# A two-layer hybrid decoder trunk: 272 projection columns moved from fifth to second place, ones multiplied ahead of the first slab, and float32r rows of 1/rms

## The chip, the cores and the metric

The kernel runs on one core of one Trainium2 chip (trn2). The metric is device time of one launch in microseconds (us), and the runs of the kernel before have a median of 1244.14 us (three runs, 1243.88 to 1245.17).

## The reference

The input is one sequence of 512 tokens with 1024 features, in float32, and it goes through two layers. Layer 0 mixes tokens by gated linear attention (GLA) and by differential attention side by side, layer 1 by dilated window attention; each is followed by a gated MLP. Only layer 0's mixer and the norms matter here:

```python
h = rmsnorm(x, norm_mix[0])
z = h @ w_in                                  # 1024 x 3088 columns
aq, ak, av, ag, ar, bq, bk, bv = split(z)     # 256,256,512,512,16,512,512,512
log_a = log_sigmoid(ar @ w_a2 + b_a) / 16     # decay of the GLA
oa = rmsnorm(gla(aq, ak, av, log_a)) * silu(ag)
ob = rmsnorm(diff_attention(norm(bq), norm(bk), bv, lam))
x = x + concat(oa, ob) @ w_out
x = x + mlp(rmsnorm(x, norm_ffn[0]))          # up to 2*2816, conv of 3, silu gate, down
```

## The kernel before, in words

**Products.** Every weight is split on the chip into a high and a low float32r half (hi by ScalarE, line 177; lo by VectorE, line 180), and so is every activation (hhi by line 204, hlo by line 205). A product is three passes: high times high, low times high, high times low. Weights come in slabs of at most 1088 columns per partition, three buffers each of raw, hi and lo. `slab()` hands out the next one and issues the load of the one two places further, so the order of `weight_slabs()` (line 94) is also the order of the weight transfers on SyncE's queue.

**Layer 0's projection.** `tok_gemm` (lines 303 to 320) makes 512, 272 or 256 columns for all 512 tokens, in four groups of 128 tokens with a PSUM bank each. It goes slab by slab, in each slab token group by token group. A 512-column product has four slabs of 24 matmuls, a 272- or 256-column one has two slabs of 48. The order before (lines 694 to 701) is: bv, bq, bk, aq with ak, half of ag with ar (the 272 columns), av, the other half of ag (256 columns). The last one's final eviction is followed by a Silu of the whole gate on ScalarE (line 686) and by the reload of the table for Ln and Exp (line 687).

**The order of TensorE's work** is written out by hand with a planner. `now` is a planned time; each step of a projection adds its planned cost (`PASS` is 0.216 us for 512 columns), and after each step all small pieces of attention that have come due are issued (`fire`). A piece is put on the list by the piece before it, with a delay in planned time:

```python
FILL, SLOPE, DTR, DPV = 1.2, 0.55, 5.5, 2.5
at(DTR, lambda: diff_tr(n, h, pr[0]), "diff")
at(FILL + SLOPE * (n + 1), lambda: diff_scores(i + 1), "diff")
```

The differential attention is one chain of 16 steps (four token blocks n of four heads), which starts after the transposes of bk. A step has scores (line 493), the transposes of its weights 5.5 later (line 515; ScalarE copies them out, line 518) and the product with bv 2.5 after that (line 527). After a block's fourth head its output is copied out (line 532), normed (lines 348 to 356 and 473) and 7.5 later transposed (line 362) and split. The block n = 3 also starts the GLA chain: `gla_sums` (line 595; ScalarE's exponentials in lines 600 and 601, VectorE's products in lines 606 to 616), `gla_tr` 5.0 later (transposes), `gla_att` (line 631), `gla_out` (lines 659 to 670). The decay needs three small pieces for each token group, `decay1` to `decay3` (lines 557, 565 and 584), started by the eviction of the 272 columns (line 551). Before the first half of the output projection (line 332) stands `drain("diff")`, before its second half `drain("gla")`:

```python
def drain(tag):
    while any(e[2] == tag for e in events):
        e = heapq.heappop(events)
        now[0] = max(now[0], e[0])
        e[3]()
```

It issues every listed piece in order of its due time until none of the tag is left, with no projection step between them. The order on ScalarE and VectorE is not written by hand: a scheduler at build time sets it.

**The start.** x is loaded in eight chunks of 128 features (256 KB each), and the first two are split at once; the first weight slab is loaded and split in two halves, of one chunk each.

**The rows of 1/rms.** Before each MLP the summed squares (128 partitions x 512 tokens, `sqacc`) are added over partitions by one float32 matmul with ones (line 251), whose result goes through a reciprocal root to all rows. It is issued after the first two up-projections (line 720, 48 matmuls).

Of the kernel before, what the change touches and what calls it, by code (L numbers as in the profile page):

```python
# [16 lines left out]
F32 = mybir.dt.float32  # L17
F32R = mybir.dt.float32r
# [6 lines left out]
P = 128  # L25
S = 512
D = 1024
DC = D // P
NT = S // P
# [48 lines left out]
def weight_slabs():  # L78


    slabs = []

    def tok(w, c0, n):
        nk = 2 if n == 512 else 4
        slabs.extend((w, 0, k * P, nk, c0, n) for k in range(0, DC, nk))

    def ffn(i):
        for gi, (f0, n) in enumerate(GROUPS):

            for j in range(f0 + (gi > 0), f0 + n + (gi < 2)):  # L90
                slabs.extend(("ffn_w_up", i, 0, DC, half + j * P, P) for half in (0, DFF))
            slabs.extend(("ffn_w_down", i, f0 * P, n, c * P, P) for c in range(DC))

    for c0, n in ((2576, 512), (1552, 512), (2064, 512), (0, 512), (1280, 272), (512, 512), (1024, 256)):
        tok("ev_w_in", c0, n)
    for r0 in (512, 0):
        slabs.extend(("ev_w_out", 0, r0, 4, c0, 256) for c0 in range(0, D, 256))
    ffn(0)
    for g, kind in ((0, 0), (0, 1), (1, 0), (1, 1), (2, 0), (2, 1), (0, 2), (1, 2), (2, 2)):
        tok("od_w_in", g * 1536 + kind * 512, 512)  # L100
    slabs.extend(("od_w_out", 0, 0, 4, c0, 256) for c0 in range(0, D, 256))
    ffn(1)
    return slabs
# [24 lines left out]
def trunk_kernel(ctx: ExitStack, tc: tile.TileContext, x, weights, params, lqks, w_a2, consts, out):  # L128
    nc = tc.nc
    V, A, G, T = nc.vector, nc.scalar, nc.gpsimd, nc.tensor  # L130

    per = ctx.enter_context(tc.tile_pool(name="per", bufs=1))
# [3 lines left out]
    ps = ctx.enter_context(tc.tile_pool(name="ps", bufs=8, space=PSUM))  # L136
# [4 lines left out]
    def bank():  # L141
        return ps.tile([P, 512], F32, name="bank")
# [64 lines left out]
    def rsqrt(dst, ss, scale, work=None):  # L207
# [7 lines left out]
        V.scalar_tensor_tensor(out=u, in0=u, scalar=-0.5, in1=a, op0=ALU.mult, op1=ALU.mult)  # L215
        V.scalar_tensor_tensor(out=dst, in0=u, scalar=1.5, in1=y, op0=ALU.add, op1=ALU.mult)

    def to_h(c, gain):
        split(hhi[:, c], hlo[:, c], xT[:, c], gain[:, c:c + 1])

    sqacc = [None]
# [23 lines left out]
                self.r = per.tile([P, NT], F32, name="rstd4", bufs=2)  # L245
                rsqrt(self.r, self.pb[:, :NT], 1.0 / D)

    def rstd_rows():

        pb = bank()  # L250
        T.matmul(pb, ones.to_broadcast([P, P]), sqacc[0], start=True, stop=True)
        bc = per.tile([P, S], F32, name="rstd_bc", tag="row", bufs=1)
        a, y, u = (tmp.tile([P, S], F32, name="qn", bufs=3) for _ in range(3))
        rsqrt(bc, pb, 1.0 / D, (a, y, u))
        return bc
# [34 lines left out]
    def run(steps):  # L290
        for us in steps:
            pe(us)
            fire()
# [6 lines left out]

    PASS = 0.216 / 512

    def tok_gemm(n, lhs, evict, before=None):

        ps = [bank() for _ in range(NT)]
        nsl = 4 if n == 512 else 2
        kper = DC // nsl
        for s in range(nsl):
            whi, wlo = slab()
            if before is not None:  # L310
                before(s)
            for t in range(NT):
                for k in range(kper):
                    kc = s * kper + k
                    for j, (a, b) in enumerate(((hhi, whi), (hlo, whi), (hhi, wlo))):
                        T.matmul(ps[t][:, :n], lhs(a[:, kc], t), b[:, k, :n],  # L316
                                 start=(kc == 0 and j == 0), stop=(kc == DC - 1 and j == 2))
                if s == nsl - 1:
                    evict(t, ps[t])
                yield 3 * kper * n * PASS  # L320

    def nat(v, t):
        return v[:, t * P:(t + 1) * P]
# [76 lines left out]
    with tc.tile_pool(name="m0", bufs=1) as m0, tc.tile_pool(name="t0", bufs=2) as t0:  # L400
# [34 lines left out]
        nc.sync.dma_start(prm, params[:, :38])  # L435
        for i in range(4):
            for c in (2 * i, 2 * i + 1):
                nc.sync.dma_start(xT[:, c], x[c])
                if i == 0:
                    to_h(c, gmix[0])  # L440
                    if c == 0:
                        load_next()
            if i in (1, 2):
                load_next()
# [246 lines left out]

            at(8.0, lambda: scaled(bv, r0)(t, ps), "params")

        run(tok_gemm(512, nat, late, before))
        run(tok_gemm(512, nat, qk_evict(qT, g_dqk, 8, r0, "diff")))
        run(tok_gemm(512, nat, qk_evict(kT, None, 8, r0, "diff", after_k)))
        run(tok_gemm(512, nat, scaled(aqk, r0)))
        run(tok_gemm(272, nat, agr_evict))
        oahi, oalo = t8("oahi", F32R), t8("oalo", F32R)
        run(tok_gemm(512, nat, scaled(av, r0, then=landing)))  # L700
        run(tok_gemm(256, nat, agr1_evict))
# [11 lines left out]
    def ffn(i, done):  # L713
        with tc.tile_pool(name=f"f{i}", bufs=2) as fp:
            def up(j):
                whi, wlo = slab()
                ps = bank()
                for kc in range(DC):
                    for m, (w, r) in enumerate(((whi, hhi), (wlo, hhi), (whi, hlo))):
                        T.matmul(ps, w[:, kc], r[:, kc], start=(kc == 0 and m == 0),  # L720
                                 stop=(kc == DC - 1 and m == 2))
                pe(3 * DC * 512 * PASS)
                return ps

            def conv3(ps, j, name):
                u = fp.tile([P, S], F32, name="u" + name)
                c = fp.tile([P, S], F32, name="c" + name)
                V.tensor_tensor(out=u, in0=ps, in1=bc, op=ALU.mult)
                cw = [conv[:, i, q, j:j + 1] for q in range(4)]
                A.activation(c, u, AF.Identity, bias=cw[3], scale=cw[2])  # L730
                V.scalar_tensor_tensor(out=c[:, 1:], in0=u[:, :S - 1], scalar=cw[1], in1=c[:, 1:], op0=ALU.mult,
                                       op1=ALU.add)
                V.scalar_tensor_tensor(out=c[:, 2:], in0=u[:, :S - 2], scalar=cw[0], in1=c[:, 2:], op0=ALU.mult,
                                       op1=ALU.add)
                return c

            ghi, glo = {}, {}

            def gate(j, pg, pv):
                cg = conv3(pg, j, "g")  # L740
                cv = conv3(pv, NF + j, "v")
                silu = A.activation(cg, cg, AF.Silu)
                if j == NF - 1:
                    tc.keep_in_program_order(A.preload_act_table_set(LN_EXP))
                V.tensor_tensor(out=cv, in0=cg, in1=cv, op=ALU.mult)  # L745
                ghi[j] = fp.tile([P, S], F32R, name="ghi", bufs=10)
                glo[j] = fp.tile([P, S], F32R, name="glo", bufs=10)
                split(ghi[j], glo[j], cv, None)

            def chunk(j):  # L750
                pg = up(j)
                gate(j, pg, up(NF + j))
                fire()

            def down(gi):
                f0, n = GROUPS[gi]
                last = gi == len(GROUPS) - 1

                def part(c, w, ps, ks, ts=slice(0, S)):
                    for k in ks:  # L760
                        for m, (a, b) in enumerate(((w[0], ghi), (w[1], ghi), (w[0], glo))):
                            T.matmul(ps[:, ts], a[:, k], b[f0 + k][:, ts], start=(k == 0 and m == 0),  # L762
                                     stop=(k == n - 1 and m == 2))
                    pe(3 * len(ks) * (ts.stop - ts.start) * PASS)

                def end(c, ps, ts=slice(0, S)):
                    V.tensor_tensor(out=xT[:, c, ts], in0=xT[:, c, ts], in1=ps[:, ts], op=ALU.add)  # L767
                    if last:
                        done(c, ts)


                first = min(LEAD, DC) if last else 0
                pend = []
                for c in range(first):
                    w, ps = slab(), bank()
                    part(c, w, ps, range(n - 1))
                    pend.append((c, w, ps))
                for c, w, ps in pend:
                    part(c, w, ps, (n - 1,))
                    end(c, ps)  # L780
                for c in range(first, DC):
                    w = slab()

                    parts = 2 if last and i == 1 and c == DC - 1 else 1
                    for q in range(parts):
                        ps, ts = bank(), slice(q * S // parts, (q + 1) * S // parts)
                        part(c, w, ps, range(n), ts)
                        fire()
                        end(c, ps, ts)

            p0 = up(0), up(NF)
            bc = rstd_rows()
            p1 = up(1), up(NF + 1)
            gate(0, *p0)
            gate(1, *p1)
            for gi, (f0, n) in enumerate(GROUPS):
                for j in range(f0 + (1 if gi else 2), f0 + n + (gi < 2)):
                    chunk(j)
                down(gi)
# [206 lines left out]
```

## Time and profile before

| | |
|---|---|
| median of three runs | 1244.14 us |
| time of the profiled execution | 1244.83 us |
| its span, first to last instruction | 1242.7 us |
| TensorE busy (matmuls) | 1230.5 us, 99% |
| VectorE busy | 765.5 us, 62% |
| ScalarE busy | 542.7 us, 44% |
| DMA, mean over the span | 92 GB/s |

Times in the profile are microseconds from the span's start. PE is TensorE's matmuls, DVE is VectorE, ACT is ScalarE. Ends of matmuls are modelled and overlap the next start, so the distance between starts says what one costs. An instruction's duration includes latency: on DVE and ACT the next one often starts some 0.1 us before the end.

### The profile page before, as it was taken

The page shows a single profiled execution, that of the slowest core. Times are in us where ns is not written, and L with a number is a line of the kernel's source. Part 1 is how long each engine was busy: PE and PEld are TensorE (multiplying, and loading weights), DVE is VectorE, ACT ScalarE, POOL GpSimd, SP SyncE. Part 2 cuts the span into 40 slices and gives each one's busy share as a digit, 9 for nine tenths or more (in the row PEclk, how much of TensorE's full clock was granted, in tenths as well). Part 3 has the DMA queues.
Part 4 walks back from the last instruction along what each step waited for, and adds up shares of the span by engine and source line. Part 5 has one row for each costly group of instructions (what it writes and reads, how often), then busy time and mean ns, then how long its engine had stood idle before and what let it go on. Part 6 is the DMA issues. An engine that isn't in the chain of part 4 may idle for free.

```text
span 1242.7 us, 15158 instructions
## 1 busy us (share of the span) xinstructions
PE 1230.5 (99%) x5870; PEld 1021.5 (82%) x5870; DVE 765.5 (62%) x1405; ACT 542.7 (44%) x891; POOL 16.5 (1%) x35
## 2 busy tenths in 40 slices
PE   8999999999999999999999999999999999999998
PEld 6887788888888888888888888889888888888887
DVE  6457768777753776366845565543787536773673
ACT  5446554454432443234634554444544324442341
POOL 0000000000000000000000000300000000000000
PEclk9999999999999999999999999999999999999999
DMA  7222121223323332332422223421223323333322
GB/s 249 89 87 68 35 65 38 85 85 102 103 88 99 102 99 88 102 98 64 136 85 87 85 68 102 106 83 51 93 94 102 102 88 99 102 93 94 102 76 93
DMA packets 34487, 114.56 MB, mean 92 GB/s; under 512 B 4423, under 2 KB 5096, under 8 KB 34416
## 3 DMA queue, kind: packets, MB, share of 16 engines
q1 hardware_dynamic: 32256, 110.38, 28.0%
q10 hardware_dynamic: 1296, 2.10, 0.5%
q0 software_dynamic: 864, 1.12, 0.4%
q8 instruction: 46, 0.75, 0.3%
q14 instruction: 25, 0.20, 0.0%
HBM read 110.41 MB, written 2.12 MB: 91 GB/s over the span
## 4 chain that ended last, share of the span: by engine, by line
PE 96%; DVE 2%; DMA 1%; ACT 1%; issue 0%; POOL 0%; SPq 0%; DVEq 0%; ACTq 0%; POOLq 0%
PE bank L720 39%; PE bank L316 26%; PE bank L762 19%; PE bank L332 5%; PE bank L362 2%; PE bank L943 1%; PE bank L493 1%; PE bank L527 1%; PE bank L928 1%; PE bank L866 1%; PE bank L855 0%; PE bank L515 0%; DMA xT<-in_xT_dram 0%; DVE lo L180 0%; ACT p L499 0%; PE bank L584 0%
## 5 line engine op out<-in xcount | busy, mean ns | idle before, releaser
L177 ACT ACTIVATE hi<-raw 128x1024 fp32r<-128x1024 f32 (+2 forms) x209 | 217.1, 1040 | 324.1 <-PE bank L762 143.2
L180 DVE TENSOR_TENSOR lo<-raw,hi 128x1024 fp32r<-128x1024 f32 (+2 forms) x209 | 250.6, 1199 | 155.9 <-ACT hi L177 148.5
L720 PE MATMUL bank<-hhi,hi 128*128 128x512 f32 x704 | 274.7, 390 | 0.0
L720 PE MATMUL bank<-hlo,hi 128*128 128x512 f32 x704 | 273.9, 389 | 0.0
L720 PE MATMUL bank<-hhi,lo 128*128 128x512 f32 x704 | 273.9, 389 | 0.0
L316 PE MATMUL bank<-hi,hhi 128*128 128x512 f32 (+2 forms) x512 | 201.6, 394 | 5.7 <-ACT hi L177 5.5
L316 PE MATMUL bank<-lo,hhi 128*128 128x512 f32 (+2 forms) x512 | 194.7, 380 | 0.0
L316 PE MATMUL bank<-hi,hlo 128*128 128x512 f32 (+2 forms) x512 | 194.4, 380 | 0.0
L720 PEld LDWEIGHTS bank<-hhi,lo 128*128 128x128 f32 x704 | 132.1, 188 | 28.1 <-issue 0.5
L720 PEld LDWEIGHTS bank<-hhi,hi 128*128 128x128 f32 x704 | 132.1, 188 | 27.8 <-issue 0.5
L720 PEld LDWEIGHTS bank<-hlo,hi 128*128 128x128 f32 x704 | 132.1, 188 | 27.4
L762 PE MATMUL bank<-ghi,lo 128*128 128x512 f32 (+1 forms) x358 | 138.0, 385 | 0.0
L762 PE MATMUL bank<-glo,hi 128*128 128x512 f32 (+1 forms) x358 | 138.0, 385 | 0.0
L762 PE MATMUL bank<-ghi,hi 128*128 128x512 f32 (+1 forms) x358 | 138.0, 385 | 0.0
L316 PEld LDWEIGHTS bank<-hi,hhi 128*128 128x128 f32 x512 | 97.3, 190 | 23.1 <-ACT hi L177 5.5
L316 PEld LDWEIGHTS bank<-lo,hhi 128*128 128x128 f32 x512 | 97.0, 190 | 18.7 <-DVE lo L180 0.2
L316 PEld LDWEIGHTS bank<-hi,hlo 128*128 128x128 f32 x512 | 97.4, 190 | 16.2 <-DVE hlo L205 0.5
L767 DVE TENSOR_TENSOR xT<-xT,bank 128x512 f32<-128x512 f32 (+1 forms) x49 | 33.1, 676 | 106.4 <-PE bank L762 106.1
L762 PEld LDWEIGHTS bank<-ghi,lo 128*128 128x128 f32 x358 | 67.2, 188 | 13.6
L762 PEld LDWEIGHTS bank<-ghi,hi 128*128 128x128 f32 x358 | 67.2, 188 | 13.5
L762 PEld LDWEIGHTS bank<-glo,hi 128*128 128x128 f32 x358 | 67.2, 188 | 13.4
L201 ACT ACTIVATE ghi<-cv 128x512 fp32r<-128x512 f32 x44 | 27.8, 631 | 109.4 <-DVE cv L745 109.4
(192 smaller groups left out, 1288.4 us busy)
## 6 DMA issues: line engine op xcount, KB each, us to landing
raw<-in_weights_dram SPq DMA_DIRECT2D x189, 512.0 KB, 3.5
raw<-in_weights_dram SPq DMA_DIRECT2D x16, 384.0 KB, 3.1
xT<-in_xT_dram SPq DMA_DIRECT2D x8, 256.0 KB, 5.3
out_dram<-xT ACTq DMA_DIRECT2D x7, 256.0 KB, 2.0
raw<-in_weights_dram SPq DMA_DIRECT2D x2, 544.0 KB, 3.6
vt<-vs POOLq DMA_DIRECT2D x16, 64.0 KB, 4.1
raw<-in_weights_dram SPq DMA_DIRECT2D x2, 256.0 KB, 3.5
tr<-in_consts_dram SPq DMA_DIRECT2D x1, 256.0 KB, 4.4
```

The costliest lines, as they stand in the source:

```text
L177: r = A.activation(hi[:, c0:c1], raw[:, c0:c1], AF.Copy)
L180: V.tensor_tensor(out=lo[:, c0:c1], in0=raw[:, c0:c1], in1=hi.bitcast(F32)[:, c0:c1], op=ALU.subtract)
L201: A.activation(hi, src, AF.Copy)
L316: T.matmul(ps[t][:, :n], lhs(a[:, kc], t), b[:, k, :n], start=(kc == 0 and j == 0), stop=(kc == DC - 1 and j == 2))
L332: T.matmul(ps, w[:, k, d * P:(d + 1) * P], r(k), start=(k == 0 and j == 0), stop=(k == nk - 1 and j == 2))
L362: T.transpose(pt[:, h * P:(h + 1) * P], src[:, h * P:(h + 1) * P], ident)
L493: T.matmul(sc[:, :nk], qT[rs, h, n * P:(n + 1) * P], kT[rs, h, :nk], start=True, stop=True)
L527: T.matmul(po[n][:, h * P:(h + 1) * P], wT[:, j * P:(j + 1) * P], bv[:, j, h * P:(h + 1) * P], start=(h == 0 and j == 0), stop=(h == 3 and ...
L720: T.matmul(ps, w[:, kc], r[:, kc], start=(kc == 0 and m == 0), stop=(kc == DC - 1 and m == 2))
L762: T.matmul(ps[:, ts], a[:, k], b[f0 + k][:, ts], start=(k == 0 and m == 0), stop=(k == n - 1 and m == 2))
L767: V.tensor_tensor(out=xT[:, c, ts], in0=xT[:, c, ts], in1=ps[:, ts], op=ALU.add)
L866: T.matmul(sc[:, hs], q[:, h, ts], k[:, h, ts], start=(h == 0), stop=(h == 3))
```

## The change

Layer 0's 272 columns are projected second, behind bv, and their two weight slabs stand second in the list of transfers. Nine matmuls of 512 columns on a tile of ones are issued ahead of everything. In the first slab of bv the order is chunk by chunk (each chunk for all token groups) with the low half of the weights second, and the first chunk of x is loaded and split in two halves of 256 tokens. The sums over partitions ahead of the MLPs are two float32r matmuls on a high and a low half of `sqacc`, which ScalarE and VectorE split first.

```diff
-    for c0, n in ((2576, 512), (1552, 512), (2064, 512), (0, 512), (1280, 272), (512, 512), (1024, 256)):
+    for c0, n in ((2576, 512), (1280, 272), (1552, 512), (2064, 512), (0, 512), (512, 512), (1024, 256)):
         tok("ev_w_in", c0, n)
...
+    V.memset(hhi[:, DC - 1].bitcast(F32), 1.0)
+    warm = bank()
+    for _ in range(9):
+        T.matmul(warm, hhi[:, DC - 1, :P], hhi[:, DC - 1], start=True, stop=True)
+    onesr = per.tile([P, P], F32R, name="onesr")
+    V.memset(onesr.bitcast(F32), 1.0)
...
-    def rstd_rows():
+    def rstd_rows(hi, lo):
         pb = bank()
-        T.matmul(pb, ones.to_broadcast([P, P]), sqacc[0], start=True, stop=True)
+        split(hi, lo, sqacc[0], None)
+        for i, v in enumerate((hi, lo)):
+            T.matmul(pb, onesr, v, start=(i == 0), stop=(i == 1))
...
+            by_chunk = chunkwise and s == 0
+            for step in range(kper * NT // 2):
+                for u in range(2):
+                    k, t = divmod(2 * step + u, NT) if by_chunk else ((2 * step + u) % kper, (2 * step + u) // kper)
                     kc = s * kper + k
+                    for j, (a, b) in enumerate(((hhi, whi), (hhi, wlo), (hlo, whi)) if by_chunk else
+                                               ((hhi, whi), (hlo, whi), (hhi, wlo))):
...
+                    if s == nsl - 1 and k == kper - 1:
+                        evict(t, ps[t])
+                if by_chunk or (2 * step + 2) % kper == 0:
+                    yield 3 * (2 if by_chunk else kper) * n * PASS
...
-                nc.sync.dma_start(xT[:, c], x[c])
-                if i == 0:
-                    to_h(c, gmix[0])
-                    if c == 0:
+                for t in ((slice(0, 2 * P), slice(2 * P, S)) if c == 0 else (slice(0, S),)):
+                    nc.sync.dma_start(xT[:, c, t], x[c, :, t])
+                    if i == 0:
+                        split(hhi[:, c, t], hlo[:, c, t], xT[:, c, t], gmix[0][:, c:c + 1])
+                    if c == 0 and t.start == 0:
                         load_next()
...
-        run(tok_gemm(512, nat, late, before))
+        run(tok_gemm(512, nat, late, before, chunkwise=True))
+        run(tok_gemm(272, nat, agr_evict))
         run(tok_gemm(512, nat, qk_evict(qT, g_dqk, 8, r0, "diff")))
         run(tok_gemm(512, nat, qk_evict(kT, None, 8, r0, "diff", after_k)))
         run(tok_gemm(512, nat, scaled(aqk, r0)))
-        run(tok_gemm(272, nat, agr_evict))
```

## Rows read from the trace of the kernel before

**Rows 1.** The page: busy time in us, share of the span, instructions.

```profile
PE 1230.5 (99%) x5870; PEld 1021.5 (82%) x5870; DVE 765.5 (62%) x1405; ACT 542.7 (44%) x891; POOL 16.5 (1%) x35
```

**Rows 2.** The waits of PE: waiter, releaser, us in total, times, longest.

```profile
PE bank L515 <- DVE p L505: 1.4, 1, 1.4
PE bank L631 <- DVE xT L338: 0.8, 1, 0.8
```

**Rows 3.** The timeline, 0 to 16 us: start, duration, engine, line, operation, out<-in.

```profile
1.10 0.17 DVE L464 MEMSET ar<- 128x128 f32 x1
...
5.47 0.80 PE L316 MATMUL bank<-hi,hhi 128*128 128x512 f32 x1 [5.47 <-ACT hi L177]
...
8.17 0.79 PE L316 MATMUL bank<-hi,hlo 128*128 128x512 f32 x1
...
10.77 1.23 DVE L180 TENSOR_TENSOR lo<-raw,hi 128x1024 fp32r<-128x1024 f32 x1 [0.80 <-ACT hi L177]
...
13.87 0.40 PE L316 MATMUL bank<-lo,hhi 128*128 128x512 f32 x1
...
15.49 0.39 PE L316 MATMUL bank<-hi,hhi 128*128 128x512 f32 x1
```

**Rows 4.** The chain that ended last, one piece: start, us, what.

```profile
30.03 27.32 PE bank L316 x120
```

**Rows 5.** The timeline ahead of the first MLP, DVE and PE.

```profile
257.25 0.68 DVE L230 TENSOR_TENSOR sqacc<-sqacc,sq 128x512 f32<-128x512 f32 x1
...
264.26 1.02 PE L251 MATMUL bank<-sqacc,cst 128*128 128x512 f32 x2
...
265.36 0.40 PE L720 MATMUL bank<-hhi,lo 128*128 128x512 f32 x1
```

**Rows 6.** The timeline at the eviction of the 272 columns' first token group.

```profile
116.40 0.29 PE L316 MATMUL bank<-lo,hhi 128*128 128x272 f32 x1
...
116.73 0.27 ACT L551 ACTIVATE ar<-bank,rstd 128x16 f32<-128x16 f32 x1 [0.86 <-PE bank L316]
```

**Rows 7.** The timeline of PE, 173 to 229 us.

```profile
173.73 1.05 PE L527 MATMUL bank<-bv,wT 128*128 128x128 f32 x8
174.54 0.36 PE L316 MATMUL bank<-hi,hhi 128*128 128x256 f32 x1
...
176.05 1.12 PE L595 MATMUL bank<-la,tri 128*128 128x256 f32 x8
...
190.12 0.28 PE L316 MATMUL bank<-lo,hhi 128*128 128x256 f32 x1
...
228.43 0.60 PE L362 MATMUL bank<-cst,qn 128*128 128x128 f32 x4
```

**Rows 8.** The timeline of ACT, 175 to 220 us.

```profile
175.23 0.59 ACT L532 ACTIVATE o<-bank 128x512 f32<-128x512 f32 x1
...
190.32 1.06 ACT L177 ACTIVATE hi<-raw 128x1024 fp32r<-128x1024 f32 x1 [1.74 <-PE bank L316]
...
191.64 0.59 ACT L664 ACTIVATE o<-bank 128x512 f32<-128x512 f32 x1
192.25 1.28 ACT L686 ACT_TABLE_LOAD   x1
...
195.47 1.28 ACT L687 ACT_TABLE_LOAD   x1
...
219.94 0.60 ACT L664 ACTIVATE o<-bank 128x512 f32<-128x512 f32 x1 [1.18 <-PE bank L661]
```

**Rows 9.** The timeline of DVE, 178 to 231 us.

```profile
178.64 0.48 DVE L610 SCALAR_TENSOR_TENSOR qs<-eb,cst,aqk 128x256 f32<-128x256 f32 x1
...
179.85 0.68 DVE L473 TENSOR_TENSOR qn<-o,rr 128x512 f32<-128x512 f32 x1
...
225.11 0.69 DVE L473 TENSOR_TENSOR qn<-o,rr 128x512 f32<-128x512 f32 x1
...
229.79 0.75 DVE L205 SCALAR_TENSOR_TENSOR oalo<-bank,prm,oahi 128x512 fp32r<-128x512 f32 x1 [0.47 <-ACT oahi L204]
```

More of the change, by code (lines that the diff above doesn't have):

```diff
@@ L301, in trunk_kernel, with tok_gemm @@
     PASS = 0.216 / 512
-    def tok_gemm(n, lhs, evict, before=None):
+    def tok_gemm(n, lhs, evict, before=None, chunkwise=False):
         ps = [bank() for _ in range(NT)]
@@ L311, in tok_gemm @@
                 before(s)
-            for t in range(NT):
-                for k in range(kper):
+            by_chunk = chunkwise and s == 0
+            for step in range(kper * NT // 2):
+                for u in range(2):
+                    k, t = divmod(2 * step + u, NT) if by_chunk else ((2 * step + u) % kper, (2 * step + u) // kper)
                     kc = s * kper + k
-                    for j, (a, b) in enumerate(((hhi, whi), (hlo, whi), (hhi, wlo))):
+                    for j, (a, b) in enumerate(((hhi, whi), (hhi, wlo), (hlo, whi)) if by_chunk else
+                                               ((hhi, whi), (hlo, whi), (hhi, wlo))):
                         T.matmul(ps[t][:, :n], lhs(a[:, kc], t), b[:, k, :n],
                                  start=(kc == 0 and j == 0), stop=(kc == DC - 1 and j == 2))
-                if s == nsl - 1:
-                    evict(t, ps[t])
-                yield 3 * kper * n * PASS
+                    if s == nsl - 1 and k == kper - 1:
+                        evict(t, ps[t])
+                if by_chunk or (2 * step + 2) % kper == 0:
+                    yield 3 * (2 if by_chunk else kper) * n * PASS
     def nat(v, t):
@@ L791, in ffn @@
             p0 = up(0), up(NF)
-            bc = rstd_rows()
+            bc = rstd_rows(*(fp.tile([P, S], F32R, name=f"sq{x}", bufs=1) for x in ("hi", "lo")))
             p1 = up(1), up(NF + 1)
```

## The prediction, made before the changed kernel ran

> **What bounds the kernel now.** The page first: TensorE (PE) has matmuls in 99% of the span [rows 1], so only what PE does differently can move the end, and an edit elsewhere counts by the wait that it makes or ends on PE. Next the rate: in a dense stretch a pass of 512 columns costs 27.32 / 120 = 0.228 us [rows 4]. Then what is lost against that rate. The list of PE's waits has, once PE has started, only two of 0.8 us or more: 1.4 us before transposes of differential attention and 0.8 us before a GLA product [rows 2]. The timeline of the start shows the largest loss: first product at 5.47, and up to 13.87 passes 0.43 to 0.44 apart ((13.87 - 8.17) / 13), with some gaps; after that 0.23 apart [rows 3]. Per 512 columns these are TensorE's levels of 1.2 and 2.4 GHz. The first slab, 24 passes, takes PE until 15.49 instead of 5.5 us. So the change can win about 4 us at the start and 2 us of waits, and has to be searched for waits that it makes.
>
> **The start.** Memset of ones: 128x128 takes 0.17 [rows 3], four times the columns at most 0.7; DVE is free at 0.85, so the first product of ones starts near 1.4. Nine at 0.43 end near 5.3, when the first real one can start (5.47 before). When does the clock rise? In rows 3 it rose 8.4 us after the first product, and 5.7 us after the row of products became unbroken. The new row is unbroken from 1.4, so between 7.1 and 9.8; I take 7.1, as it is the unbroken row that is alike. Then 4 passes until 7.1 and 20 at 0.228 end the first slab at 11.7. The second slab needs its low weights from its third pass on, at 10.77 + 1.23 = 12.0 [rows 3], which just fits. Gain 15.49 - 11.7 = 3.8; one more issue on SyncE's queue may land later chunks some tenths later: **3.6 us** taken. Ends: 3.9 (bound by the low weights at 12.0, whatever the clock) and 2.5 (rise at 9.8: 10 passes before it, 14 after, end at 13.0). The smaller pieces of x on ACT and DVE are hidden behind transfers.
> The Trainium skill, "TensorE: Matmul & The Clock Gate", section "What's actually happening", says that the clock is held down until activity releases it, by a monitor that runs freely beside the kernel; by it the rise varies from run to run, and an early one would give the 3.9.
>
> **Rows of 1/rms.** The float32 matmul holds PE from 264.26 to 265.36, less one pass of 0.23 that started in between: 0.87 us [rows 5]. Two float32r passes cost 0.46. Twice: **0.8 us** gained. The split (ACT and DVE, 0.7 each) can run from 257.9 on, 5 us earlier than needed [rows 5], behind the two up-projections; without that cover it would cost 1.4 a time.
>
> **The 272 columns.** Their matmuls and the decay's small products cost PE the same wherever they stand, and their two weight slabs only swap places in SyncE's queue. What changes is who covers whom.
> (a) The 1.4 us wait lies where decay pieces and attention share ACT and DVE; the 0.8 us one is explained below. With decay gone from there and GLA shifted I take both as ended: **2.2 gained** (0 to 2.5).
> (b) Behind bv nothing else is interleaved, so by the delays `decay1(0)` and `decay1(1)` come directly after the step whose eviction they need. Last pass at 116.40, eviction from 116.73 for 0.27 [rows 6]: 0.6 from start to end, of which 0.13 is the pass: **0.95 lost** for the two (0 to 1.5); the other two stand behind a `decay2`.
> (c) The chain of differential attention loses cover. I followed the planner, whose order for the kernel before is the trace's order. From the end of bk's product it now has 16 + 16 + 8 steps ahead (20.7 + 20.7 + 10.4) plus the chain's own pieces and seven transposes (32.5): 84.3 planned us. The last product with bv is due 86.8 after that end. Before, it was issued with all 8 steps of the 256-column product still ahead (173.73, then the first of them at 174.54) [rows 7]; the 272 columns were 11 us of cover, the decay pieces 3.3. So now all steps are used up when the last transposes of weights are issued, and `drain("diff")` issues in a row: last product with bv, `gla_sums`, `gla_tr`, next `gla_sums`, last output transposes; then the output projection, which needs the split of these. This is what is late next, and everything on PE is queued behind it.
> I lay this on the rows before, zero being the end of the last 256-column step (190.24). ACT there first converts a weight slab, evicts, makes one copy (191.64 to 192.2), then is taken by table load, Silu and table load until 195.47 + 1.28 = 196.75 [rows 8]; that block delayed the GLA's copies and made the 0.8 us wait. The copy's place falls to the last weights: the product with bv waits until 2.0 (transposes end at 0.4). With it and `gla_sums` PE is busy to 3.8. But the attention output and the exponentials need ACT, free at 6.5. Before, from the start of the output copy (175.23) it took 3.9 to the last GLA operand (178.64 + 0.48) and 5.3 to the normed output (179.85 + 0.68) [rows 8, 9]. So operands at 10.4, `gla_tr` and `gla_sums` to 11.8, output transposes then, and 2.1 from their start to the low half, as at 228.43 to 229.79 + 0.75 [rows 7, 9]; the first two passes of the projection precede that half: projection from 13.45. PE's own work in this is 4.35, so **9.1 us idle**. Without the Silu block in the way the output copy starts at 3.1 instead of 6.5: 5.7; without the slab conversion too: 4.8. Ends 3.0 (bare latencies: two copies 1.2, products and transposes 2.4, seven small DVE and ACT steps 2.4, split 1.4, less PE's work) and 10.5.
> (d) `drain("gla")` too: the last transposes now come two steps (5.4) and a transpose after the last `gla_out`, with nothing behind them. That norm takes 225.11 + 0.69 - 219.94 = 5.9 from its copy [rows 8, 9], so 0.3 wait, and the split after them costs 2.1 less 0.4 less two passes, 1.2: **1.5 lost** (0.5 to 2.5); before, a step of projection followed them.
>
> **Sum.** -3.6 - 0.8 - 2.2 + 0.95 + 9.1 + 1.5 = **+4.95 us** on the profiled execution's 1244.83: 1249.8. That execution is 0.7 over the median, so **1249.1**. About 0.2% (2.5 us) is what a measurement of this kernel can tell from no change.
>
> **Rivals.**
> 1. The Silu block is placed elsewhere by the build-time scheduler (nothing pins it to that spot, and its result is needed only some 15 us later); idle 5.7 or 4.8: +1.5 or +0.6, so 1245 to 1246. Against it: Silu is ready exactly then and ACT has nothing else. Chance 0.22.
> 2. Faster, if the drain is near bare latency: with nothing else on DVE, idle is 3.0; with 3.9 for the start: -3.9 - 0.8 - 2.2 + 0.95 + 3.0 + 0.5 = -2.5 and with `decay1` hidden -3.4, so 1240.7 to 1241.6. It decides where the drain idles under 4 us. Chance 0.15.
> 3. In the drain PE stands still from 3.8 to about 9.5, longer than anywhere after 13.87, so no row says whether the clock holds. If it falls to the 1.2 GHz level, passes cost 0.43 until it rises; by the 5.7 us of rows 3 that is 13 passes, 2.6 us more, and some 0.7 on the small products: 1252.4. Chance 0.17. The Trainium skill, same page, section "Why this matters for your kernels", speaks for it: pauses between bursts let the clock drop; by it the sum would be this one.
> 4. The ones don't do what they are for: the clock rises where it did, gain 0: 1252.7. Chance 0.08; the row of products before the rise was shorter in rows 3 than it will be.
>
> **Numbers.** Forecast 0.38, rivals as above. Slower is forecast, 3 and 4: 0.63; same is rival 1: 0.22; faster rival 2: 0.15. The range reaches from inside rival 2 over the forecast with its bounds to rivals 3 and 4 with one bound more (a drain of 10.5): 1241.3 to 1254.5.
>
> **What would show it.** Right: matmuls of ones from about 1.4, passes 0.23 apart from 7 on, second slab near 11.7; line 251's successor at two passes of 0.23; PE waits of about 2 us before the last product with bv and 5 us or more before the GLA transposes, with ACT in table load and Silu; the 1.4 us wait gone; and the first MLP starting some 5.7 us later than before. Wrong: PE gapless between the 256-column product and the output projection, or the Silu behind the output copy.

## The result, and the profile after

The changed kernel takes 1258.09 us (median of 4 runs, 1257.77 to 1258.35), the kernel before 1244.03 us beside it. The ratio is 1.0111, 95% interval 1.0093 to 1.0128: 14 us slower. The forecast was slower, but by 5 us (1249.1), and the range ended at 1254.5. The profiled execution has 1258.25 us and a span of 1256.5, 13.8 more than before.

Lines of before have moved: the projection's matmuls are L330 (L316 before), the output projection L347 (L332), the transposes L377 (L362), the weights' transposes and the product with bv L531 and L543 (L515, L527), `gla_sums` L611 (L595), the decay's first matmul L573 (L557), the Silu and the table load behind it L702 and L703 (L686, L687), the first up-projection L736 (L720).

The page of the changed kernel, two lines: busy time of TensorE, and the granted clock in 40 slices.

```profile
PE 1237.6 (99%) x5879; PEld 1026.4 (82%) x5879; DVE 767.8 (61%) x1410; ACT 545.0 (43%) x894; POOL 16.5 (1%) x35
...
PEclk9999998999999999999999999999999999999999
```

PE still fills 99% of the span [rows 1]. It has 7.1 us more of matmul time. The nine products of ones are 4.2 of them, and the first slab's passes at full clock and the cheaper sums take some off again, so matmuls got slower somewhere else. The clock line says where: the seventh slice (188 to 220 us) holds an 8.

The waits of PE in the changed kernel (waiter, releaser: us in total, times, longest).

```profile
PE bank L377 <- DVE rs_a L211: 5.2, 1, 5.2
PE bank L377 <- DVE qn L489: 1.8, 1, 1.8
PE bank L573 <- ACT ar L567: 1.6, 3, 0.9
PE bank L222 <- DVE hhi L219: 1.5, 1, 1.5
PE bank L543 <- ACT wT L534: 1.4, 1, 1.4
PE bank L347 <- ACT oahi L204: 1.3, 1, 1.3
PE bank L347 <- ACT ohi L204: 0.8, 1, 0.8
PE bank L347 <- DVE oalo L205: 0.6, 1, 0.6
```

Both waits of [rows 2] are gone. In their place stand 12.7 us (the list without the 1.5 before the first product): 7.4 around `drain("diff")` (5.2, 1.4, 0.8), 1.6 before the decay's first matmuls, 1.9 behind `drain("gla")` (1.3, 0.6), and 1.8 before transposes in the middle of the output projection.

The timeline of the changed kernel around `drain("diff")`, PE and ACT (start, duration, engine, line, operation, out<-in, shapes, in brackets the wait before).

```profile
182.44 0.60 PE L531 MATMUL bank<-cst,p 128*128 128x128 f32 x4
...
183.84 0.58 ACT L534 ACTIVATE wT<-bank 128x512 f32<-128x512 f32 x1
184.44 1.28 ACT L702 ACT_TABLE_LOAD   x1
184.47 1.16 PE L543 MATMUL bank<-bv,wT 128*128 128x128 f32 x8 [1.44 <-ACT wT L534]
...
185.73 1.91 ACT L702 ACTIVATE ag<-ag 128x2048 f32<-128x2048 f32 x1
187.66 1.28 ACT L703 ACT_TABLE_LOAD   x1
188.96 0.60 ACT L548 ACTIVATE o<-bank 128x512 f32<-128x512 f32 x1
...
191.75 1.09 PE L377 MATMUL bank<-cst,ks 128*128 128x128 f32 x4 [5.17 <-DVE rs_a L211]
...
195.19 1.06 PE L377 MATMUL bank<-cst,qn 128*128 128x128 f32 x4
197.02 0.80 PE L347 MATMUL bank<-ohi,hi 128*128 128x512 f32 x1 [0.78 <-ACT ohi L204]
...
198.92 0.63 PE L347 MATMUL bank<-ohi,hi 128*128 128x512 f32 x1
199.34 0.63 PE L347 MATMUL bank<-ohi,lo 128*128 128x512 f32 x1
...
201.01 0.39 PE L347 MATMUL bank<-olo,hi 128*128 128x512 f32 x1
201.24 0.39 PE L347 MATMUL bank<-ohi,hi 128*128 128x512 f32 x1
```

This is the drain as it was laid out in the prediction: no projection step between 182.44 and 197.02, ACT in table load, Silu and table load from 184.44 to 188.94, the copy of the attention output behind them, and PE at rest meanwhile. New are the durations behind the 5.17 us: transposes take 1.06 to 1.09 us for four where four took 0.60 before the wait, and the passes of the output projection stand 0.42 to 0.43 apart from 198.92 to 200.62 and 0.23 from 201.01 on (the first three, 0.59 to 0.71 apart, contain a wait as well). The granted clock is half from 190.71 to 200.95: PE runs at its level of 1.2 GHz there, instead of 2.4.

The same stretches by windows (us; length, then busy us of PE, PEld, DVE, ACT and POOL with instruction counts, granted clock as a share of 2.4 GHz, DMA share, GB/s): first of the changed kernel,

```profile
190.00:200.00 10.00, 7.40 (x26) 5.93 (x27) 7.67 (x21) 3.42 (x8) 0.52 (x1) 0.54 0.01 2
200.00:210.00 10.00, 10.00 (x67) 9.03 (x67) 5.45 (x10) 3.11 (x5) 0.53 (x1) 0.95 0.07 9
210.00:220.00 10.00, 10.00 (x73) 9.17 (x72) 9.94 (x32) 3.25 (x7) 1.07 (x2) 1.00 0.12 45
220.00:230.00 10.00, 8.16 (x59) 7.36 (x58) 9.94 (x27) 3.13 (x6) 0.00 (x0) 1.00 0.16 53
...
240.00:250.00 10.00, 8.10 (x30) 6.06 (x29) 4.25 (x7) 1.80 (x3) 0.00 (x0) 0.83 0.16 52
```

then of the kernel before.

```profile
200.00:210.00 10.00, 10.00 (x73) 9.14 (x72) 9.91 (x24) 3.70 (x6) 1.05 (x2) 1.00 0.16 54
210.00:220.00 10.00, 9.81 (x75) 8.94 (x74) 9.78 (x29) 3.71 (x9) 0.00 (x0) 1.00 0.00 1
220.00:230.00 10.00, 10.00 (x49) 8.27 (x48) 8.19 (x16) 3.28 (x6) 0.00 (x0) 1.00 0.25 65
```

Two things were not in the prediction's sum. The clock is below full in two places, 190 to 201 and again in 240 to 250. And PE loses 1.84 us between 220 and 230, where VectorE is full (9.94 of 10). A full VectorE alone is not new: before, where the GLA's outputs came 11 to 17 us earlier, it was as full from 200 to 220 (9.91 and 9.78), and PE lost 0.2 us there.

The second place, timeline of PE in the changed kernel from the last output transposes on:

```profile
241.71 0.60 PE L377 MATMUL bank<-cst,qn 128*128 128x128 f32 x4
243.59 0.50 PE L347 MATMUL bank<-oahi,hi 128*128 128x512 f32 x1 [1.28 <-ACT oahi L204]
...
244.94 0.50 PE L347 MATMUL bank<-oalo,hi 128*128 128x512 f32 x1 [0.62 <-DVE oalo L205]
245.27 0.58 PE L347 MATMUL bank<-oahi,hi 128*128 128x512 f32 x1
...
248.91 0.40 PE L347 MATMUL bank<-oahi,hi 128*128 128x512 f32 x1
```

After waits of only 1.28 and 0.62 us the nine passes from 245.27 to 248.91 take 3.64 us; at 0.228 [rows 4] they would take 2.05.

The start of the changed kernel, same view, PE with one row each of ACT and DVE:

```profile
1.46 4.21 PE L222 MATMUL bank<-hhi 128*128 128x512 f32 x9 [1.46 <-DVE hhi L219]
...
6.59 0.40 PE L330 MATMUL bank<-hi,hhi 128*128 128x512 f32 x1
...
11.03 1.04 ACT L177 ACTIVATE hi<-raw 128x1024 fp32r<-128x1024 f32 x1
...
12.11 1.23 DVE L180 TENSOR_TENSOR lo<-raw,hi 128x1024 fp32r<-128x1024 f32 x1 [0.67 <-ACT hi L177]
12.13 0.50 PE L330 MATMUL bank<-hi,hhi 128*128 128x512 f32 x1
...
13.39 0.50 PE L330 MATMUL bank<-lo,hhi 128*128 128x512 f32 x1 [0.52 <-DVE lo L180]
```

The clock rises at 6.4 and the second slab begins at 12.13 instead of 15.49 [rows 3], but its third pass, which needs the low weights, waits until 13.39. The gain that is left is 2.4 us: the transposes of the first row of 1/rms (L242) start at 26.67 instead of 29.09.

Last the sums of 1/rms ahead of the first MLP, same view:

```profile
278.88 0.39 PE L261 MATMUL bank<-sqhi,onesr 128*128 128x512 f32 x1
279.11 0.39 PE L261 MATMUL bank<-sqlo,onesr 128*128 128x512 f32 x1
```

Two passes 0.23 apart, no wait. The first MLP begins at 268.00 instead of 253.38, 14.6 us later; at the last matmul (1252.73, before 1238.86) the distance is 13.9. So the whole loss lies before 268, and 0.75 us is won back behind it, where the two sums are.

### The profile page after: what moved, and what is told of

It reads as the page before. It is cut to its first block, busy times and chain, and to the rows that moved or that the text cites. A ratio compares the mean times of both kernels' runs of the same rounds, so it can differ in the third digit from the quotient of the medians.

```text
span 1256.5 us, 15185 instructions
## 1 busy us (share of the span) xinstructions
PE 1237.6 (99%) x5879; PEld 1026.4 (82%) x5879; DVE 767.8 (61%) x1410; ACT 545.0 (43%) x894; POOL 16.5 (1%) x35
## 4 chain that ended last, share of the span: by engine, by line
PE 94%; DVE 2%; ACT 1%; DMA 1%; issue 0%; SPq 0%; POOL 0%; DVEq 0%; POOLq 0%; ACTq 0%
PE bank L736 38%; PE bank L330 25%; PE bank L778 19%; PE bank L347 5%; PE bank L377 2%; PE bank L959 1%; PE bank L509 1%; PE bank L543 1%; PE bank L944 1%; PE bank L882 1%; PE bank L871 0%; DVE lo L180 0%; DMA xT<-in_xT_dram 0%; PE bank L531 0%; ACT hi L177 0%
## 5 line engine op out<-in xcount | busy, mean ns | idle before, releaser
L736 PE MATMUL bank<-hhi,hi 128*128 128x512 f32 x704 | 274.0, 389 | 0.0
L736 PE MATMUL bank<-hlo,hi 128*128 128x512 f32 x704 | 274.0, 389 | 0.0
L736 PE MATMUL bank<-hhi,lo 128*128 128x512 f32 x704 | 274.0, 389 | 0.0
L330 PE MATMUL bank<-hi,hhi 128*128 128x512 f32 (+2 forms) x512 | 201.1, 393 | 0.4 <-ACT hhi L204 0.4
L330 PE MATMUL bank<-lo,hhi 128*128 128x512 f32 (+2 forms) x512 | 194.1, 379 | 0.5 <-DVE lo L180 0.5
L330 PE MATMUL bank<-hi,hlo 128*128 128x512 f32 (+2 forms) x512 | 193.1, 377 | 0.0
L736 PEld LDWEIGHTS bank<-hhi,lo 128*128 128x128 f32 x704 | 132.2, 188 | 27.5
L736 PEld LDWEIGHTS bank<-hhi,hi 128*128 128x128 f32 x704 | 132.2, 188 | 27.4
L736 PEld LDWEIGHTS bank<-hlo,hi 128*128 128x128 f32 x704 | 132.2, 188 | 27.2
L330 PEld LDWEIGHTS bank<-lo,hhi 128*128 128x128 f32 x512 | 96.3, 188 | 19.5 <-DVE lo L180 1.3
L330 PEld LDWEIGHTS bank<-hi,hhi 128*128 128x128 f32 x512 | 96.8, 189 | 17.6 <-issue 1.0
L330 PEld LDWEIGHTS bank<-hi,hlo 128*128 128x128 f32 x512 | 96.8, 189 | 15.5 <-DVE hlo L205 0.2
L778 PEld LDWEIGHTS bank<-glo,hi 128*128 128x128 f32 x358 | 67.3, 188 | 13.3
```

What stands on the lines that cost most here:

```text
L330: T.matmul(ps[t][:, :n], lhs(a[:, kc], t), b[:, k, :n], start=(kc == 0 and j == 0), stop=(kc == DC - 1 and j == 2))
```

## The experiments

The theory: the move of the 272 columns costs 16 to 18 us, through waits in the two drains and the clock that falls behind them; the other three parts gain 2 to 3. Rivals: the ones, the split chunk of x or the chunkwise slab cost something, or the waits alone do it and the clock doesn't matter.

### The move alone: `move_only`

The kernel before with the columns moved, nothing else.

```diff
-    for c0, n in ((2576, 512), (1552, 512), (2064, 512), (0, 512), (1280, 272), (512, 512), (1024, 256)):
+    for c0, n in ((2576, 512), (1280, 272), (1552, 512), (2064, 512), (0, 512), (512, 512), (1024, 256)):
...
         run(tok_gemm(512, nat, late, before))
+        run(tok_gemm(272, nat, agr_evict))
...
-        run(tok_gemm(272, nat, agr_evict))
```

> The kernel before with the 272 columns second and nothing else of the change. Theory (lost cover): all of the loss comes from the move, about 17 us up to the first MLP by the two traces (14.6 later there in spite of 2.4 won at the start), so 1260 to 1262 us, with the same waits behind the last 256-column step and TensorE at the lower clock level for some us. Rival (the earlier start disturbs transfers or the order on ScalarE and VectorE, and that is much of the loss): 1250 to 1255.

Measured: 1261.05 us (1258.98 to 1262.96), ratio 1.0140 (1.0123 to 1.0156). The list of its PE's waits has the new ones of the changed kernel at the same places (5.2, 1.9, 1.6, 1.4, 1.3, 0.8, 0.6), and the clock is half from 191.09 to 197.92 and from 245.70 to 249.12. All of the loss is the move's.

### All but the move: `no_move`

The changed kernel with the columns fifth again, as before.

```diff
-    for c0, n in ((2576, 512), (1280, 272), (1552, 512), (2064, 512), (0, 512), (512, 512), (1024, 256)):
+    for c0, n in ((2576, 512), (1552, 512), (2064, 512), (0, 512), (1280, 272), (512, 512), (1024, 256)):
...
-        run(tok_gemm(272, nat, agr_evict))
         run(tok_gemm(512, nat, qk_evict(qT, g_dqk, 8, r0, "diff")))
...
         run(tok_gemm(512, nat, scaled(aqk, r0)))
+        run(tok_gemm(272, nat, agr_evict))
```

> The changed kernel with the 272 columns back in fifth place. Theory: 2.4 us of the start and 0.8 us of the rows of 1/rms remain, 1240.5 to 1241.5 us, and the kernel is faster than before. Rival (the other parts lose too): 1244 or more.

Measured: 1241.51 us (1240.85 to 1242.14), ratio 0.9978 (0.9969 to 0.9987). The first MLP begins at 251.04, 2.3 us earlier than before. In the list of PE's waits the two of [rows 2] are back, and none of the drains' is there:

```profile
PE bank L531 <- DVE p L521: 1.4, 1, 1.4
PE bank L647 <- DVE xT L353: 0.8, 1, 0.8
```

So the three other parts together gain 2.8 us, and this version beats both kernels, by 0.2% against the kernel before, with an interval clear of 1. It also shows that the 2.2 us of [rows 2] come from the columns' place, as step (a) had it.

### The Silu out of the drain: `silu_late`

The changed kernel with Silu and the table load behind it on ScalarE issued after the split of the last attention output.

```diff
-            if t == NT - 1:
-                A.activation(ag.rearrange("p t d -> p (t d)"), ag.rearrange("p t d -> p (t d)"), AF.Silu)
-                tc.keep_in_program_order(A.preload_act_table_set(LN_EXP))
...
+        def gate_silu():
+            flat = ag.rearrange("p t d -> p (t d)")
+            tc.keep_in_program_order(A.activation(flat, flat, AF.Silu))
+            tc.keep_in_program_order(A.preload_act_table_set(LN_EXP))
...
             drain(("diff", "gla")[half])
+            if half == 0:
+                gate_silu()
```

> The changed kernel with the Silu of the gate and its two table loads put behind the split of the last attention output on ScalarE. Theory (that block is 4.5 us on the path of the drain): the wait of 5.2 us before the GLA transposes shrinks to about 2, and the clock no longer falls there, 1251 to 1254 us. Rival (VectorE's norm and operands set the wait): 1256.5 to 1258.5.

Measured: 1253.13 us (1252.77 to 1253.51), ratio 1.0071 (1.0056 to 1.0086), 5.0 less than the changed kernel. Its timeline of PE:

```profile
188.29 0.63 PE L377 MATMUL bank<-cst,ks 128*128 128x128 f32 x4 [1.88 <-DVE rs_a L211]
...
192.64 0.50 PE L347 MATMUL bank<-ohi,hi 128*128 128x512 f32 x1 [0.78 <-ACT ohi L204]
```

The 5.17 us wait is 1.88, the output projection begins at 192.64 instead of 197.02, and the clock is low for 3.41 us in all (194.35 to 197.76) instead of 13.65; the expectation had no fall left. So the block on ACT held the chain up by 3.3 us of wait, and in this trace most of the low clock is gone with it.

### The clock by itself: `fill18`

The changed kernel with 18 matmuls of 512 columns, whose result nothing reads, put where PE stands still. The output doesn't change.

```diff
+            if n == 0:
+                hold = bank()
+                for _ in range(18):
+                    T.matmul(hold, hhi[:, 0, :P], hhi[:, 0], start=True, stop=True)
             at(5.0, lambda: gla_tr(n, ks, qs, kd), "gla")
```

> The changed kernel with 18 more 512-column matmuls (4.1 us at the high level) that nothing reads, issued in the 5.2 us wait of the drain, between the first sums of the GLA and the transposes. Theory (the fall of the clock in that wait costs about 3 to 4 us by itself): the clock holds until the output projection and the time falls to 1254 to 1255.5. Rival (the low clock is hidden under the waits for VectorE and ScalarE): 1257.5 to 1258.5, or more if the extra matmuls delay something.

Measured: 1255.58 us (1255.25 to 1256.71), ratio 1.0088 (1.0073 to 1.0103). Its timeline of PE:

```profile
186.06 4.27 PE L636 MATMUL bank<-hhi 128*128 128x512 f32 x18
...
195.75 0.50 PE L347 MATMUL bank<-ohi,hi 128*128 128x512 f32 x1 [0.78 <-ACT ohi L204]
```

The chain is about as long as in the changed kernel, but the clock stays full until the last microsecond of this run and doesn't fall even after the waits of 1.3 and 0.6 behind `drain("gla")`, which stand in its list too. The first MLP begins at 263.98, 4.0 earlier than in the changed kernel. So adding 18 matmuls saves time: 2.5 us by the medians. In the two traces 2.9 of the 4.0 reach the last matmul (1249.80 against 1252.73); a wait of 1.3 us in the last layer (L948), which is 0.2 in the changed kernel, accounts for the difference.

### Between the two places: `fourth`, `fourth_decay4`, `fourth_feed`

The columns fourth, behind bk: the chain has its cover back, and the decay is early all the same.

```diff
-    for c0, n in ((2576, 512), (1280, 272), (1552, 512), (2064, 512), (0, 512), (512, 512), (1024, 256)):
+    for c0, n in ((2576, 512), (1552, 512), (2064, 512), (1280, 272), (0, 512), (512, 512), (1024, 256)):
...
-        run(tok_gemm(272, nat, agr_evict))
...
         run(tok_gemm(512, nat, qk_evict(kT, None, 8, r0, "diff", after_k)))
+        run(tok_gemm(272, nat, agr_evict))
```

> The changed kernel with the 272 columns fourth, directly behind bk. They then cover the chain of differential attention again, but the decay pieces still come earlier than before. Theory (what counts is the number of projection steps behind bk): within 2 us of the kernel with fifth place, 1240 to 1243. Rival (early decay work or the order of the weight transfers is what hurts): 1250 to 1258.

Measured: 1251.57 us (1249.72 to 1255.92), ratio 1.0063 (1.0042 to 1.0084). A miss, with a time in the rival's range: the 5.2 us wait is gone, but the time isn't back, and the list has a new wait of 1.9 us before the GLA's product in L675. Its timeline of PE:

```profile
94.87 0.28 PE L573 MATMUL bank<-cst,ar 128*32 128x128 f32 x1 [1.49 <-ACT ar L567]
...
96.13 1.63 PE L600 MATMUL bank<-cst,y 128*128 128x2 f32 x8
...
98.30 0.63 PE L330 MATMUL bank<-hi,hlo 128*128 128x512 f32 x1
...
113.48 0.41 PE L330 MATMUL bank<-hi,hlo 128*128 128x512 f32 x1
```

The clock fell at 96.42, among the decay's small products behind a wait of 1.49 us, and stayed at half until 113.49, though PE was busy all through: 17.07 us at half, worth 8.5. The next two runs tried to take its cause away. First the wait, with the decay's first piece due 4.0 instead of 1.0 after the eviction:

```diff
-            at(1.0, lambda: decay1(t), "gla")
+            at(4.0, lambda: decay1(t), "gla")
```

> The kernel with the 272 columns fourth, in which the first decay piece comes 4.0 instead of 1.0 planned us after its eviction. Theory (the fourth place has its cover; its 10 us over the fifth came from the clock, which fell at 96 for 17 us right after a 1.5 us wait of decay transposes for their eviction): the wait is gone, the clock holds, 1241.5 to 1244. Rival (short decay products between 272-column steps bring the clock down without a wait): 1249 to 1252.

Measured: 1251.26 us (1250.71 to 1254.44), ratio 1.0057 (1.0042 to 1.0072). No wait over 0.7 us is left in that stretch, and the clock falls all the same (at 102.66 and 109.49, 3.41 us each, and twice later, behind waits of 2.7 us in L675 and 1.3 us in the output projection). The rival was right: the wait is not the cause, or not alone. Then two unread passes of 512 columns in each `decay2` and `decay3` of `fourth`, to keep the array loaded between the small products (the output doesn't change):

```diff
+        def feed():
+            hold = bank()
+            for _ in range(2):
+                T.matmul(hold, hhi[:, 0, :P], hhi[:, 0], start=True, stop=True)
```

> The kernel with the 272 columns fourth, with two more 512-column matmuls that nothing reads in each of the eight decay2 and decay3 pieces (16 passes, 3.6 us of TensorE). Theory (too few columns pass in the stretch of 272-column steps, decay pieces and first scores, and this lets the clock fall): the clock holds, 1251.6 - 8.5 + 3.6, so 1245 to 1248. Rival (something else brings it down, such as the waits): it falls as before, 1251 to 1256.

Measured: 1252.36 us (1247.66 to 1254.34), ratio 1.0061 (1.0038 to 1.0083). In one of four runs the clock held, with the time that the theory gave (1247.66); in the others it fell (in the profiled one at 96.79, for 6.83 us). Not conclusive: what brings the clock down in this stretch stays open.

### The chain issued earlier: `second_fill05`, `second_fill02`

The columns second, as in the changed kernel, but the chain's steps planned closer together, so that it ends before the projections do.

```diff
-        FILL = 1.2
+        FILL = 0.5
```

> The changed kernel (272 columns second) in which the planner's time between two score steps of differential attention is 0.7 shorter (FILL 0.5 instead of 1.2), so that the chain is 11 planned us shorter and ends, by the planner, before the last 256-column step is used up. Theory (lost cover is the cause, and a shorter chain gives it back): the waits of the first drain and the fall of the clock there are gone, only the second drain's waits of about 2 us stay, 1242 to 1246. Rival (VectorE and ScalarE can't follow the shorter steps, or the place itself costs): 1249 or more.

Measured: 1249.92 us (1249.17 to 1250.70), ratio 1.0046 (1.0029 to 1.0062). Its list of PE's waits begins with a new one, 2.7 us for `att` before the GLA's product in L675. It ends at 202.65, in the output projection, and the clock is half from 202.73 to 206.14 and once more at 236.86. The drain's wait is gone, and the next one decides; the time is the rival's.

With `FILL = 0.2`:

> As the run with FILL 0.5, with FILL 0.2: by the planner neither drain idles. Theory: 1240.5 to 1243.5, near or under the kernel with fifth place. Rival (waits of the score steps for ScalarE and VectorE take the place of those in the drains): 1244 to 1249.

Measured: 1246.83 us (1245.69 to 1247.43), ratio 1.0018 (1.0008 to 1.0027). The longest waits of PE behind the start are 3.4 us in three before output transposes (L377, for `qn`) and the decay's 1.6. The clock never falls in its trace, and both drains are free of waits. That is 11.3 us under the changed kernel with nothing moved back, and shows from the other side that missing cover was the loss. But the chain now runs into itself: 2.5 of the 3.4 us are one wait before output transposes at 145.27, and the time is the rival's, not the theory's 1240.5 to 1243.5. With the columns fifth and `FILL` as it was it is 1241.51; so the move gains nothing in any form tried. Fifth place with `FILL = 0.2` was not run.

### The start: `x_whole`, `no_move_x_whole`, `no_move_no_ones`

The first chunk of x in one piece, in the changed kernel and in `no_move`:

```diff
-                for t in ((slice(0, 2 * P), slice(2 * P, S)) if c == 0 else (slice(0, S),)):
+                for t in (slice(0, S),):
```

> The changed kernel with the first chunk of x loaded and split in one piece. Theory (the halves make all later transfers land about 1 us later, as the conversion of the second slab started at 10.7 to 11.0 in four traces with halves and at 9.7 and 10.2 in two without): the second slab starts up to 1 us earlier, 1256.8 to 1257.5. Rival (the halves pay, since the first matmuls start on half a chunk): 1258 to 1259.

> The changed kernel with the 272 columns back in fifth place and the first chunk of x in one piece. Theory: 0.5 to 1 us under the kernel with fifth place, 1240.5 to 1241. Rival (the halves pay or do nothing): 1241.5 to 1242.

Measured: 1257.02 us (1256.21 to 1258.32) and 1241.07 (1240.49 to 1242.09), ratios 1.0096 (1.0079 to 1.0113) and 0.9971 (0.9960 to 0.9982). Both are lower than with the halves, by 1.1 and 0.4 us, and in neither pair do the intervals come apart. The second slab's conversion starts at 10.69 and 10.13; in the changed kernel and `no_move` it is 11.03, but other traces with the halves have it as early as 10.53. So the halves bring nothing that can be seen, and may cost some tenths. The second of the two is the best median of the study.

The ones taken out of `no_move` (memset and nine matmuls):

```diff
-    V.memset(hhi[:, DC - 1].bitcast(F32), 1.0)
-    warm = bank()
-    for _ in range(9):
-        T.matmul(warm, hhi[:, DC - 1, :P], hhi[:, DC - 1], start=True, stop=True)
```

> The changed kernel with the 272 columns back in fifth place and without the nine matmuls of ones. Theory (the ones bring the rise of the clock from 10 to 14 us forward to 5 to 8 us): 1.5 to 2.4 us slower than with them, 1243 to 1244. Rival (transfers and conversions set the start anyway): 1241.5 to 1242.5.

Measured: 1241.96 us (1241.32 to 1242.92), ratio 0.9980 (0.9970 to 0.9989), 0.45 more than with them. Timeline of PE without the ones:

```profile
9.77 0.63 PE L326 MATMUL bank<-hi,hhi 128*128 128x512 f32 x1
10.20 0.45 PE L326 MATMUL bank<-lo,hhi 128*128 128x512 f32 x1
```

The clock rises at 10.3 instead of 5.4, yet only tenths of this reach the end. With the ones PE stands until 13.40 for the low weights of the second slab; without them the same pass starts at 13.93, and PE waits for no weights in that slab. So the weights leave half a microsecond for the ones to win, and the rival's time came out. Without the ones the first MLP still begins at 251.37, 2.0 us earlier than before.

## Why the prediction was wrong in size

The sum of the prediction, term by term, with what the runs showed. It comes to 13.95 us, against 13.87 at the last matmul.

| term | predicted | measured | from |
|---|---|---|---|
| start | -3.6 | -2.4 | 29.09 to 26.67 |
| rows of 1/rms | -0.8 | -0.75 | 14.62 less 13.87 |
| (a) waits of [rows 2] | -2.2 | -2.2 | gone; back in `no_move` |
| (b) `decay1` | +0.95 | +1.6 | list of waits |
| (c) `drain("diff")`, clock with it | +9.1 | +12.4 | 10.2 + 2.2 |
| (d) `drain("gla")`, out-projection, clock | +1.5 | +5.3 | 1.84 + 1.28 + 0.62 + 1.6 |

**Right: cover, drains, Silu.** From the last 256-column step (182.44) to the output projection (197.02) are 14.6 us; the prediction had 13.45. In `fill18`, where the clock held, it is 13.7 (the step ends 0.36 earlier). So the length of the bare chain was right within 0.3 us (13.7 against 13.45), and `move_only`, `no_move` and `silu_late` show that the reason was right too: the columns were the chain's cover, and the Silu block lies on its path. Rival 1 (the block placed elsewhere) and rival 2 (faster) fall.

**(c): the step that failed is that the clock holds.** It stood in the sum as no cost and beside it as rival 3, with a chance of 0.17 and a price of 2.6 + 0.7 us. The clock did fall: 14.58 less 4.35 of PE's own work is 10.2 us, 0.9 more than the bare chain, and from 197.02 to 201.01 eight passes take 3.99 us instead of 1.82, 2.2 more. Not all of this is the clock: counted from the last 256-column step, the eight passes end after 18.57 us here and after 16.52 in `fill18`, so the clock's price is 2.05 us, less than the rival's 3.3. The other 1.0 is in `fill18` too, where the eight passes take 2.85: the third of them waits for the low half of the split (here it starts at 198.33, the low half ends at 197.53 + 0.74 = 198.27). The prediction had let two passes hide that half, which was 1.0 too little. With a rest of 5.7 us ahead and none like it in the trace of before, nothing spoke for the clock to hold; taking it as held was choosing the cheaper of two unknowns. The Trainium skill, "TensorE: Matmul & The Clock Gate", section "Why this matters for your kernels", says that pauses between bursts of matmuls let the clock drop; at this place the trace agrees (5.17 us of rest, then half clock until 200.95).

**(d): mis-sized by 3.8 us, and this took the result out of the range.** Predicted was only the tail: a norm's 0.3 and a split's 1.2. The tail's own waits came to 1.9. Not seen were two followers. The GLA's first two outputs come 7.3 us apart (207.41 and 214.73) where they were 13.3 apart before (190.24 and 203.53). The second one's norm on VectorE, for which the transposes wait 1.84, takes 10.3 us from its copy (216.79 to 227.08) instead of 8.0 (205.52 to 213.47): a weight slab's conversion (1.23) and the split of the output before it (0.74) now stand in its middle, and before they stood ahead of it. That the closer order is the cause is read from the traces; no run tested it alone. And a second fall of the clock behind the tail's waits costs 1.6. Rival 3 had one fall, in the first drain only, and no case had the GLA pressed together; without the 3.8 the time would have been 1254.3, just inside the range's end of 1254.5 (by its own terms, 1252.7 + 1.4, that end was 1254.1).

**Start: 2.4 instead of 3.6.** The clock rose earlier than taken (6.4, not 7.1), and the gain was smaller all the same. The step that failed is the low weights "at 10.77 + 1.23 = 12.0", which "just fits": it took over their time from before, but in the changed kernel they came at 12.11 + 1.23 = 13.34. The end of 2.5 in the prediction was put there for a late clock and came true for another reason. The means was misjudged as well: the prediction gave the whole gain to the ones, and rival 4 put it at 0 if they fail. The ones are worth 0.45 us by the medians, with intervals that overlap (`no_move_no_ones`), and 2.0 of the 2.3 us by which `no_move` reaches the first MLP earlier are there without them. Those 2.0 may come from the order of the first slab or from the clock's rise, which came at 10.3 there and at 13.85 in the trace of before; no run parts the two. So a gain of about the right size was in part luck. In (b) there were three waits, not two, the longest 0.9.

**Rows of 1/rms: right.** Two passes 0.23 apart, the split hidden; the 0.75 in the table is what the distance to before shrinks by behind the first MLP's start.

## What to carry to other kernels

Before moving a block of independent work, count what dependent chain it covers: work that lies behind the chain's start is its cover, and moved ahead of it the chain's tail comes out bare, though no engine has more to do. Price every rest of TensorE that the change makes with the clock at half for some time behind it, and let that be the forecast unless a row shows the clock holding over a rest as long. When a chain starts later, look also at the engine that must now do its pieces closer together.

## What the runs showed that was not expected

- **The clock's fall is not told by the wait ahead of it.** Behind `drain("gla")` the same two waits (1.3 and 0.6 us) are followed by 3.41 us at half clock in the changed kernel and `move_only`, and by none in `fill18` and `silu_late`. The 1.4 us wait of [rows 2] brought no fall. In `fourth` a wait of 1.49 us among small products was followed by 17.07 us at half clock with PE busy, and in `fourth_decay4` the clock fell with no wait over 0.7 us nearby. In `second_fill02` it held over a wait of 2.51 us.
- **The rise varies too.** In the traces with the same ones ahead it comes between 4.63 (`fourth_feed`) and 7.68 us (`fourth`), in the changed kernel at 6.39; with the start of before at 13.85 and, in `move_only`, at 10.18. So part of the late rise in the profile of before belongs to that one execution, and the ones are worth less than it suggests. The prediction had cited the Trainium skill ("TensorE: Matmul & The Clock Gate", section "What's actually happening") for a rise that varies from run to run; the traces agree that it does. That section gives ±500 ns, and here the measured spread with the ones is 3.05 us.
- **Unread matmuls can save time**: 18 of them, 4.27 us of PE, made the changed kernel 2.5 us faster.
